# Hybrid attention and recurrence block on one core: f, q and k projected with the activations stationary and turned by transposing transfers

## The chip, the cores and the metric

The kernel runs on one core of a Trainium2 chip. Its time is the device time of one execution in microseconds, as the median of several runs. On the core, PE multiplies matrices, DVE and ACT work elementwise, POOL issues some transfers here, and SP does nothing but issue transfers, one after another. Each engine takes its instructions in the order of the program and waits at an instruction until what it needs is there.

## What is computed

One layer on 256 positions of 2048 channels, all in float32. Cut to what matters here:

```python
a = rmsnorm(h, norm_mix_pre)
proj = a @ w_in                  # q, k, v of 24 heads; q, f, i, g of 8 recurrent heads; 2 gates
qh, kh = rotary(q), rotary(k)    # per head of 128: x * cos + [-x[64:], x[:64]] * sin
attn = dilated window attention in three groups of 8 heads, mixed by their softmax denominators
f = lb + (1 - lb) * sigmoid(f_r); q_h = silu(q_r)
r_out = gated linear recurrence(q_h, log f, 1 - f, i_r), normed, gated
y = sigmoid(gate_a) * (attn @ w_attn_branch) + sigmoid(gate_r) * (r_out @ w_hgrn_branch)
h = h + rmsnorm(y @ w_mix_out)
h = h + rmsnorm((silu(gate) * up) @ w_ffn_down)
```

## The kernel before

Every float32 matrix product is made of three products of halves: weight and activation are split into a high part (a rounded copy, ACT) and a low part (the rest, DVE), and high x high, high x low and low x high are added up in PSUM. The normed input lies transposed in SBUF as `xT` (channels on partitions, tokens along the row), its two parts side by side.

The weights come as a stream that a list of items orders, and one loop walks the list. An item of the first stage ("wide": g, the gates, v, i) holds 1 MB of weights. An item of the second stage is a chunk of 512 KB; two chunks are loaded into one `raw` buffer by `load_pair` (two transfers on SP). There are three `raw` buffers and three `w` buffers for the split weights. In its turn of the loop, item i does this: `prepare(i)` splits the weights of item i+2 (`split_chunk`: ACT copies the high part, DVE subtracts) and asks for a load further on; `multiply(i)` issues the matmuls; `advance(evacs)` moves the evacuation of the last finished block by one step, up to its next `yield`; `advance_lanes()` does a step of the recurrence and of the attention, which run beside the stream; `ahead_of_time(i)` issues a piece of `weight_sums`, which lays sums of weights for the feed-forward part into DRAM, by POOL. With three `w` buffers, the split of a chunk can start when PE has finished the chunk three places before it; PE then has two chunks ready.

The second stage is f, q of the recurrence, and q and k of the attention: 16 blocks of 512 columns (f twice, recurrent q twice, then for each half of the heads q and k of three groups). A block of kind "W" has the weights stationary: its product comes out transposed, with channels on partitions and tokens along the row, as recurrence and attention want them. The moving operand is `both`, high and low part of the activations together, 512 wide, and then the high part alone, 256 wide, against the low weights. Each block of 512 columns is two of 256 (`add_wide`), and `both_halves` adds the two halves of its bank. `evac_rope` then swaps halves of the partitions (ACT) and multiplies by tables that stand along the partitions. The other kind, "N", has the activations stationary and 512 columns of weights moving; the later gates and the two branches use it.

The feed-forward part already turns matrices by transposing transfers: `turn_act` splits float32 words into their 16-bit halves (ACT, L1387), lets SP transpose them (L1393), and joins the halves again two steps later (ACT, L1402).

Of the kernel before, what the change touches and what calls it, by code (L numbers as in the profile page):

```python
# [14 lines left out]
F32 = mybir.dt.float32  # L15
# [37 lines left out]
class Block:  # L53
# [7 lines left out]
    def __init__(self, kind, w, nk, col, xs, evac, pre=None, mid=None, post=None):  # L61
        self.kind, self.w, self.nk, self.col = kind, w, nk, col
# [39 lines left out]
def tile_hybrid_block(ctx: ExitStack, tc: tile.TileContext, t, out):  # L102
# [81 lines left out]
    rowb = cpool.tile([P, S], F32, name="rowb")  # L184
# [9 lines left out]
    tabs = kp.tile([P, 4, S], F32, name="tabs")  # L194
# [37 lines left out]

    def add_wide(w, nk, col, xs, ev, post=None):
        for i in range(2):
            add("W", w, nk, col + 256 * i, xs, both_halves(ev, i), post=post if i == 0 else None)

    def both_halves(ev, i):
        def go(banks):
            s = ptile("sum").rearrange("p (h t) -> p h t", h=2)
            for n, ps in enumerate(banks):  # L240
                nc.scalar.activation(s[:, n, :], ps[:, S:], AF.Copy)
            for n, ps in enumerate(banks):
                nc.vector.tensor_add(s[:, n, :], ps[:, :S], s[:, n, :])
            yield from ev(i, s)
        return go
# [50 lines left out]
    def weight_sums(jobs):  # L296

        def pieces(n):
            b, i = steps[n][:2]
            m = b.order[i][0]  # L300
            return [
                b.w[(2 * m + k) * P : (2 * m + k + 1) * P, b.cols[g] : b.cols[g] + 512]
                for g, k in product(range(2), repeat=2)
            ]

        def copy(n, lo):
            if lo == 0:
# [14 lines left out]
        for at in range(len(jobs) + 3):  # L322
            for lag in (3, 2, 1, 0):
                for part in stages[lag]:
                    if 0 <= at - lag < len(jobs):
                        part(jobs[at - lag])
                    yield
            yield
            yield
# [61 lines left out]
    def multiply_chunk(j, sides=(0, 1)):  # L391
# [4 lines left out]
        for s in sides:  # L396
            if s == 1 and c == 0 and b.mid:
                b.mid()
            for kk in range(b.per):
                k = b.per * c + kk  # L400
                first, last = k == 0, k == b.nk - 1
                xh, xl, both = b.xs(k)
                if b.kind == "N":
                    ps = b.banks[s]
                    sh, sl = (x[:, s * P : (s + 1) * P] for x in (xh, xl))
                    mm(ps, sh, wh[:, kk, :], first, False)
                    mm(ps, sh, wl[:, kk, :], False, False)
                    mm(ps, sl, wh[:, kk, :], False, last)
                    continue
                h, l = (w[:, kk, s * P : (s + 1) * P] for w in (wh, wl))  # L410
                pair = [(b.banks[s], h, both), (b.banks[s][:, :S], l, xh)]
                for i, (ps, x, y) in enumerate(pair if k % 2 == 0 else pair[::-1]):
                    mm(ps, x, y, first and i == 0, last and i == 1)
# [156 lines left out]

    class Split:
# [77 lines left out]
    def row_broadcast(dst, rc):  # L649

        ds = [small("diag", P, 2) for _ in range(2)]
        for b in range(2):
            nc.vector.tensor_scalar(ds[b], ident, rc[:, b : b + 1], None, op0=OP.mult)
        yield
        yield
        yield
        ps = aux()
        for b in range(2):
            mm(ps[:, b * P : (b + 1) * P], ones[:, :P], ds[b], True, True)
        yield  # L660
        nc.scalar.activation(dst, ps[:, :S], AF.Copy)

    def by_rows(row, n):
        return row[:, None, :].to_broadcast([P, n, S])

# [51 lines left out]
    def opening():  # L717
# [8 lines left out]
        yield from row_broadcast(rowb, r1c)  # L726
        ready.add("rowb")
        yield
        for _ in range(24):
            yield  # L730
        for i, (j, c) in enumerate(((0, -QSCALE), (1, QSCALE), (0, 1.0), (1, -1.0))):
            nc.vector.scalar_tensor_tensor(
                out=tabs[:, i, :], in0=cs[:, j, :], scalar=c, in1=rowb, op0=OP.mult, op1=OP.mult
            )
            yield
# [58 lines left out]
    def evac_f(half):  # L794
        def ev(i, src):
            while "lb" not in ready:
                yield
            if i == 0:
                fT[half] = fslot("f").rearrange("p (h t) -> p h t", h=4)
            dst = fT[half]  # L800
            d = dst[:, 2 * i : 2 * i + 2, :]
            nc.vector.tensor_mul(d, src, by_rows(rowb, 2))
            nc.scalar.activation(d, d, AF.Sigmoid)
            yield
            for h in (2 * i, 2 * i + 1):
                g = 4 * half + h
                nc.vector.tensor_scalar(
                    dst[:, h, :], dst[:, h, :], lb1[:, g : g + 1], lb[:, g : g + 1],
                    op0=OP.mult, op1=OP.add,
                )  # L810
        return ev

    def evac_qr(half, then=None):
        def ev(i, src):
            if i == 0:
                qT[half] = fslot("q").rearrange("p (h t) -> p h t", h=4)
            d = qT[half][:, 2 * i : 2 * i + 2, :]
            s = ptile("sig").rearrange("p (h t) -> p h t", h=2)
            nc.vector.tensor_mul(d, src, by_rows(rowb, 2))
            nc.scalar.activation(s, d, AF.Sigmoid)  # L820
            yield
            nc.vector.tensor_mul(d, d, s)
            if i == 1 and then:
                then()
        return ev
# [69 lines left out]
    def evac_rope(key, tab, then=None):  # L895

        cos = tabs[:, tab, :]
        sin = tabs[:, tab + 1, :]

        def ev(i, src):  # L900
            if i == 0:
                qkT[key] = fslot("qk").rearrange("p (h t) -> p h t", h=4)
            yield
            w = ptile("w").rearrange("p (h t) -> p h t", h=2)
            for o, n in ((0, 64), (64, 0)):
                nc.scalar.activation(w[o : o + 64], src[n : n + 64], AF.Copy)
            yield
            u = src
            nc.vector.tensor_mul(u, src, by_rows(cos, 2))
            nc.vector.tensor_mul(w, w, by_rows(sin, 2))  # L910
            nc.vector.tensor_add(
                qkT[key][:, 2 * i : 2 * i + 2, :].rearrange("p h (two j) -> p h two j", two=2),
                u.rearrange("p h (j two) -> p h two j", two=2),
                w.rearrange("p h (j two) -> p h two j", two=2),
            )
            if i == 1 and then:
                then()
        return ev
# [667 lines left out]
    for half in range(2):  # L1586
        add_wide(w_in, KD, COL_FR + 512 * half, xT, evac_f(half),
                 post=(lambda c: end_phase0() if c == 2 else None) if half == 0 else None)
    for half in range(2):
        add_wide(w_in, KD, COL_QR + 512 * half, xT,  # L1590
                 evac_qr(half, start_recurrence(half)))
    for half in range(2):
        for g in range(3):
            c = 1024 * g + 512 * half
            add_wide(w_in, KD, COL_Q + c, xT, evac_rope(("q", half, g), 0))
            if g == 2:
                items_pre[len(chunks)] = lambda half=half: fetch_values(half)
            add_wide(w_in, KD, COL_K + c, xT, evac_rope(("k", half, g), 2,
                     start_attention(half) if g == 2 else None))
# [3 lines left out]
    for j in range(2, 4):  # L1603
        add("N", w_in, KD, COL_GA + 512 * j, xT, evac_gate(("a", j)))
    for j in range(4):
        add("N", t["w_hgrn_branch"][0], 8, 512 * j, lambda k: recT[0](k), evac_rec_branch(j),
            pre=begin_branches if j == 0 else None)
    for j in range(4):
        add("N", t["w_attn_branch"][0], 8, 512 * j, lambda k: attnT[0](k), evac_attn_branch(j),
# [141 lines left out]
```

## Time and profile before

| what | number |
|---|---|
| median of three runs | 1689.33 us (1688.76 to 1690.47) |
| the profiled execution | 1692.25 us, its span 1690.5 us |
| granted clock of PE, mean | 0.999 |
| PE busy | 1677.3 us, 99% of the span |
| DVE busy | 1367.4 us, 81% |
| ACT busy | 982.9 us, 58% |
| moved by transfers | 419.31 MB |

A share of busy time is an average over stages. The second stage lies from 350 us to 756 us of the span. Idle time of an engine that others do not wait for costs nothing.

### The profile page before, as it was taken

Reading aid. Unit: us, or ns where it says so; the run is one execution under the profiler, and the core shown is the slowest. Engines: PE = TensorE matmul, PEld = TensorE weight load, DVE = VectorE, ACT = ScalarE, POOL = GpSimd, SP = SyncE. Lnnn points to the kernel's source line nnn. Section 1 sums busy time; section 2 is a strip of 40 time slices with the busy share of each in tenths; the row PEclk is TensorE's granted clock in tenths of the full one; section 3 lists DMA queues with packets and bytes.
Section 4 is the critical chain, followed back from the end, with each engine's and each line's share of the span. In section 5 each row is a group of like instructions: output and inputs, shape, how many; then the busy total and the mean of one; then the engine's idle time right before and its main releaser. Section 6 shows DMA issues by size and latency. Waiting matters only on the chain.

```text
span 1690.5 us, 22175 instructions
## 1 busy us (share of the span) xinstructions
PE 1677.3 (99%) x8169; PEld 1406.0 (83%) x8169; DVE 1367.4 (81%) x1543; ACT 982.9 (58%) x1102; POOL 199.9 (12%) x358
## 2 busy tenths in 40 slices
PE   9999999999999999999999999999999999999997
PEld 7888878888888888888888888888888888888886
DVE  6999888865876876665568988899888888898987
ACT  6655555544455545555545556676667666665653
POOL 0012222143443332210000000000000000000000
PEclk9999999999999999999999999999999999999999
DMA  8678989999999998865657556899888888887673
GB/s 286 206 249 279 272 270 272 272 270 254 282 247 243 297 247 214 213 219 171 218 181 265 192 194 197 271 288 269 270 265 284 273 272 273 278 275 271 238 254 131
DMA packets 257006, 419.31 MB, mean 248 GB/s; under 512 B 38352, under 2 KB 105088, under 8 KB 256896
## 3 DMA queue, kind: packets, MB, share of 16 engines
q1 hardware_dynamic: 231600, 358.73, 65.6%
q0 software_dynamic: 17984, 41.97, 12.4%
q10 hardware_dynamic: 7312, 17.18, 2.8%
q8 instruction: 64, 1.05, 0.3%
q14 instruction: 46, 0.38, 0.1%
HBM read 397.89 MB, written 56.10 MB: 269 GB/s over the span
## 4 chain that ended last, share of the span: by engine, by line
PE 83%; DMA 7%; DVE 4%; ACT 3%; issue 2%; POOL 1%; ACTq 0%; SPq 0%; DVEq 0%; POOLq 0%
PE acc L139 55%; PE aux L139 27%; DMA raw<-in_w_in 7%; DVE wl L434 2%; ACT w L432 1%; DVE e L534 1%; ACT dh L459 1%; PE aux L962 0%; POOL beats L343 0%; ACT e L849 0%; PE aux L629 0%; DVE sum L448 0%; DVE fz L1525 0%; DVE w L379 0%; ACTq L852 0%
## 5 line engine op out<-in xcount | busy, mean ns | idle before, releaser
L139 PE MATMUL acc<-xT,w 128*128 128x256 f32 (+1 forms) x2048 | 365.4, 338 | 0.2 <-DVE w L379 0.2
L434 DVE TENSOR_TENSOR wl<-raw,w 128x2048 fp32r<-128x2048 f32 (+1 forms) x140 | 304.4, 2183 | 74.3 <-ACT w L432 72.5
L379 DVE TENSOR_TENSOR w<-raw,w 128x1024 fp32r<-128x1024 f32 x176 | 215.3, 1224 | 166.7 <-ACT w L378 166.6
L139 PEld LDWEIGHTS acc<-xT,w 128*128 128x128 f32 x2048 | 311.9, 188 | 45.2 <-DVE w L379 0.6
L432 ACT ACTIVATE w<-raw 128x2048 fp32r<-128x2048 f32 (+1 forms) x140 | 254.5, 1826 | 104.2 <-DMA raw<-in_w_in 27.6
L378 ACT ACTIVATE w<-raw 128x1024 fp32r<-128x1024 f32 x176 | 186.0, 1058 | 195.3 <-PE acc L139 144.3
L139 PE MATMUL acc<-w,xT 128*128 128x512 f32 x578 | 168.9, 392 | 0.0
L453 ACT ACTIVATE w<-sum 128x1024 fp32r<-128x1024 f32 x57 | 60.6, 1063 | 168.7 <-DVE sum L448 159.0
L343 POOL COPY beats<-raw 128x1 f32<-128x1 f32 x185 | 92.2, 499 | 523.5 <-DMA raw<-in_w_in 522.9
L139 PE MATMUL acc<-w,hT 128*128 128x512 f32 x472 | 152.7, 391 | 0.4 <-DVE hT L1276 0.4
L461 DVE TENSOR_TENSOR wl<-sum,w 128x1024 fp32r<-128x1024 f32 x114 | 137.2, 1221 | 6.8 <-ACT w L453 6.7
L139 PEld LDWEIGHTS acc<-w,xT 128*128 128x128 f32 x578 | 108.2, 188 | 22.2
L139 PE MATMUL aux<-w,hT 128*128 128x512 f32 x374 | 120.0, 389 | 0.0
L139 PE MATMUL aux<-w,xT 128*128 128x512 f32 x344 | 109.9, 389 | 0.0
L463 DVE TENSOR_TENSOR dl<-raw,dh 128x1536 fp32r<-128x1536 f32 x57 | 100.2, 1757 | 11.0 <-ACT dh L459 9.4
L139 PEld LDWEIGHTS acc<-w,hT 128*128 128x128 f32 x472 | 88.5, 188 | 19.0 <-DVE hT L1276 0.9
L139 PE MATMUL acc<-wl,hT 128*128 128x512 f32 x236 | 91.8, 389 | 0.0
L459 ACT ACTIVATE dh<-raw 128x1536 fp32r<-128x1536 f32 x57 | 84.1, 1475 | 5.0 <-PE acc L139 3.2
L139 PE MATMUL acc<-w,a 128*128 128x512 f32 x268 | 83.6, 389 | 0.0
L139 PEld LDWEIGHTS aux<-w,hT 128*128 128x128 f32 x374 | 70.2, 188 | 14.5
L139 PE MATMUL acc<-w,so 128*128 128x512 f32 x240 | 80.4, 389 | 0.0
L139 PE MATMUL aux<-w,a 128*128 128x512 f32 x254 | 79.5, 389 | 0.0
(289 smaller groups left out, 3115.8 us busy)
## 6 DMA issues: line engine op xcount, KB each, us to landing
raw<-in_w_in SPq DMA_DIRECT2D x270, 512.0 KB, 6.6
raw<-in_w_ffn_gate_up SPq DMA_DIRECT2D x156, 512.0 KB, 5.1
raw<-in_w_ffn_down SPq DMA_DIRECT2D x88, 512.0 KB, 5.5
presum<-in_w_ffn_gate_up POOLq DMA_DIRECT2D x120, 256.0 KB, 6.8
s<-presum SPq DMA_DIRECT2D x40, 512.0 KB, 6.7
raw<-in_w_mix_out SPq DMA_DIRECT2D x32, 512.0 KB, 4.9
act<-acts SPq DMA_DIRECT2D x22, 512.0 KB, 6.4
presum<-presum POOLq DMA_DIRECT2D x40, 256.0 KB, 6.5
```

What stands on the lines that cost most here:

```text
L139: nc.tensor.matmul(ps, lhsT, rhs, start=start, stop=stop, skip_group_check=True)
L343: nc.gpsimd.tensor_copy(beats, ahead[:, :1])
L378: nc.scalar.activation(wh, raw, AF.Copy)
L379: nc.vector.tensor_sub(wl, raw, wh.bitcast(F32))
L432: nc.scalar.activation(hi[:, c], raw[:, c], AF.Copy)
L434: nc.vector.tensor_sub(lo[:, c], raw[:, c], hi[:, c].bitcast(F32))
L453: nc.scalar.activation(hi[:, :1024], s[:, :1024], AF.Copy)
L459: nc.scalar.activation(dhi, d, AF.Copy)
L461: nc.vector.tensor_sub(lo[:, c], s[:, c], hi[:, c].bitcast(F32))
L463: nc.vector.tensor_sub(dlo, d, dhi.bitcast(F32))
L534: add_to(b.rest[key], b.bank[key], b.rest[key])
```

## The change

All 16 blocks become kind "N", so the kind goes, with `add_wide`, `both_halves`, `row_broadcast` and the row `rowb`. A block is one of 512 columns now, in eight chunks. It comes out with tokens on partitions, so evacuation works along the row: `side` applies sigmoid, or the rotation, to 128 tokens by 512 columns, and the result is turned. For this `halves_apart` (ACT) lays the 16-bit halves of the words apart, two transposing transfers on SP turn them (one per 128 tokens), and after some yields `halves_joined` (ACT, twice) puts words together. The tables of the rotation are transposed at the start and scaled per token. `weight_sums` loses two empty steps per round, and its steps are taken at each item of the first stage, at two of five chunks at first and at every second later, until the mixing begins.

```diff
-        self.per = 4 if kind == "W" else 2
-        self.width = 1024 // self.per
+        self.per, self.width = 2, 512
...
     def ahead_of_time(i):
 
-        if back:
+        first = len(early) * KD // 2
+        turn = items[i][0] is steps or (i % 5 in (0, 2) if i < first + 8 * KD else i % 2 == 0)
+        if back and turn and i < together:
...
+    def halves_apart(flat, words):
+
+        nc.scalar.activation(
+            flat.bitcast(U16).rearrange("p (z c) -> p z c", z=2),
+            words.bitcast(U16).rearrange("p (c z) -> p z c", z=2), AF.Copy,
+        )
...
+    def by_channel(side, done, parity=False, turns_for=3):
+
+        def go(banks):
             while "lb" not in ready:
                 yield
...
+            for i in range(2):
+                halves_apart(flat[:, i, :], side(i, banks[i]))
+            for i in range(2):
+                nc.sync.dma_start_transpose(
+                    planes.rearrange("p (n t) -> p n t", n=8)[:, :, i * P : (i + 1) * P],
+                    flat[:, i, :].bitcast(U16),
+                )
+            for _ in range(turns_for):
+                yield
+            words = fslot("words")
...
+                halves_joined(words, planes.rearrange("p (z n) -> p z n", z=2))
+            done(words.rearrange("p (h t) -> p h t", h=4))
+        return go
...
+    def evac_f(half):
+        def side(i, ps):
+            d = ptile("d")
+            nc.scalar.activation(d, ps, AF.Sigmoid, scale=r1c[:, i : i + 1])
+            return d
...
+    def evac_qr(half, then):
+        def side(i, ps):
+            d, r = ptile("d"), r1c[:, i : i + 1]
+            nc.scalar.activation(d, ps, AF.Sigmoid, scale=r)
+            nc.vector.scalar_tensor_tensor(
+                out=d, in0=ps, scalar=r, in1=d, op0=OP.mult, op1=OP.mult
+            )
+            return d
...
     def evac_rope(key, tab, then=None):
...
+            nc.vector.tensor_mul(u, x, by_heads(tabs[:, tab, i, :]))
+            nc.vector.tensor_mul(w, x, by_heads(tabs[:, tab + 1, i, :]))
             for o, n in ((0, 64), (64, 0)):
...
+                nc.vector.tensor_sub(u[:, :, o : o + 64], u[:, :, o : o + 64], w[:, :, n : n + 64])
+            return u.rearrange("p h d -> p (h d)")
...
+        return by_channel(side, done, True, 2 if then else 3)
```

`then` starts the attention and is given for the last k block of each half; these two blocks are joined one chunk earlier. In the changed kernel the split is at L362 (ACT) and L363 (DVE), `load_pair` at L255, the rotation at L915 to L918, `halves_apart` at L550, the transposes at L792, `halves_joined` at L564.

On ACT, before, around the first q block of the attention's second half (`sum` is what `both_halves` adds, `w` of L906 the swapped halves, `p` and `pt` the attention's):

```order
L378 ACTIVATE w_5206<-raw_4995 128x1024
L378 ACTIVATE w_5239<-raw_5060 128x1024
L241 ACTIVATE sum_5263<-acc_5115 128x256
L241 ACTIVATE sum_5263<-acc_5116 128x256
L950 ACTIVATE p_5273,m_5274<-p_5273,m_5274 128x512
L378 ACTIVATE w_5279<-raw_5060 128x1024
L906 ACTIVATE w_5298<-sum_5263 64x512 x2
L378 ACTIVATE w_5305<-raw_5112 128x1024
L378 ACTIVATE w_5346<-raw_5112 128x1024
```

The evacuation stands in pieces of two between the copies of the splits. On ACT, now, at the same block (`flat` are the halves apart, `turn` the transposed ones, `words` the joined):

```order
L362 ACTIVATE w_4855<-raw_4665 128x1024
L362 ACTIVATE w_4870<-raw_4724 128x1024
L550 ACTIVATE flat_4890<-u_4892 128x1024
L550 ACTIVATE flat_4890<-u_4899 128x1024
L362 ACTIVATE w_4928<-raw_4724 128x1024
L957 ACTIVATE p_4947,m_4948<-p_4947,m_4948 128x512
L362 ACTIVATE w_4951<-raw_4783 128x1024
L362 ACTIVATE w_4971<-raw_4783 128x1024
L564 ACTIVATE words_4986<-turn_4891 128x1024 x2
L362 ACTIVATE w_5007<-raw_4832 128x1024
```

Both `flat` stand ahead of the copy of the next chunk but one (`w_4928`), and `words` stands ahead of `w_5007`. When `flat` is made PE has left the block; `w_4870`, `w_4928`, `w_4951`, `w_4971`, `w_5007` are the third to the seventh chunk of the block after it.

On DVE, now, at the same place (`u` and `w` of L915 to L918 belong to the rotation, `acc` is the finished bank):

```order
L363 TENSOR_TENSOR w_4870<-raw_4724,w_4870 128x1024
L915 TENSOR_TENSOR u_4892<-acc_4668,tabs 128x512
L916 TENSOR_TENSOR w_4893<-acc_4668,tabs 128x512
L918 TENSOR_TENSOR u_4892<-u_4892,w_4893 128x4x64 x2
L915 TENSOR_TENSOR u_4899<-acc_4669,tabs 128x512
L916 TENSOR_TENSOR w_4900<-acc_4669,tabs 128x512
L918 TENSOR_TENSOR u_4899<-u_4899,w_4900 128x4x64 x2
L363 TENSOR_TENSOR w_4928<-raw_4724,w_4928 128x1024
```

The whole rotation of a block stands between two splits, where before it was three operations for half a block. On SP, now, with what each waits for (DVE_49 is a count of DVE's instructions):

```order
L255 DMA raw_4832<-in_w_in 128x2x512 [waits DMAHW1_49,DMAHW2_49,DVE_49,Pool_49]
L255 DMA raw_4832<-in_w_in 128x2x512
L255 DMA raw_4873<-in_w_in 128x2x512 [waits DMAHW5_49,DMAHW3_49,DMAHW6_49,DVE_49,Pool_49]
L255 DMA raw_4873<-in_w_in 128x2x512 [waits DMAHW4_49]
L792 DMA_TRANSPOSE turn_4891<-flat_4890 128x8x128 x2
L255 DMA raw_4954<-in_w_in 128x2x512 [waits DMAHW7_49,DMAHW0_49,DVE_49]
```

Before, this queue holds loads alone here. `raw_4873` takes the buffer of `raw_4724`, so its first transfer waits until DVE has split both chunks of that buffer, `w_4928` the last; the two transposes stand behind it, and they have no wait of their own, since that one contains it.

More of the change, by code (lines that the diff above doesn't have):

```diff
@@ L231, in add @@
             chunks.append([b, c, None, None, None])
[L233 to L245, printed above, removed]
     def add_wide_block(*args, **kw):
@@ L327, in weight_sums @@
                     yield
-            yield
-            yield
     def fetch_sums(i):
@@ L401, in multiply_chunk @@
                 first, last = k == 0, k == b.nk - 1
[L402 to L413, printed above, removed]
+                ps = b.banks[s]
+                sh, sl = (x[:, s * P : (s + 1) * P] for x in b.xs(k)[:2])
+                mm(ps, sh, wh[:, kk, :], first, False)
+                mm(ps, sh, wl[:, kk, :], False, False)
+                mm(ps, sl, wh[:, kk, :], False, last)
     def split_wide(n):
@@ L568, in pair_sums, with halves_joined @@
             yield
+    def halves_apart(flat, words):
[3 more added lines that the diff above has]
+        )
+    def halves_joined(words, planes):
+        n = len(words.shape)
+        for z in range(2):
+            out = words.bitcast(U16)
+            if n == 2:
+                out = out.rearrange("p (c z) -> p z c", z=2)[:, z, :]
+            else:
+                out = out.rearrange("p h two (j z) -> p z h two j", z=2)[:, z]
+            nc.scalar.activation(out, planes[:, z], AF.Copy)
     class Split:
@@ L647, in transpose_in @@
         high(0), high(1), low(0), low(1)
[L649 to L664, printed above, removed]
     evacs, turns, lanes, queue = deque(), deque(), [deque(), deque()], deque()
@@ L725, in opening @@
         nc.scalar.preload_act_table_set("silu_and_others")
-        yield from row_broadcast(rowb, r1c)
-        ready.add("rowb")
+        for _ in range(5):
+            yield
+        ps = aux()
+        for j, i in product(range(2), repeat=2):
+            nc.tensor.transpose(
+                ps[:, (2 * j + i) * P : (2 * j + i + 1) * P], cs[:, j, i * P : (i + 1) * P], ident
+            )
         yield
-        for _ in range(24):
+        nc.scalar.activation(cs, ps.rearrange("p (j t) -> p j t", j=2), AF.Copy)
+        for _ in range(22):
             yield
[L731 to L734, printed above, removed]
+        for n, (j, c) in enumerate(((0, -QSCALE), (1, QSCALE), (0, 1.0), (1, -1.0))):
+            for i in range(2):
+                nc.vector.tensor_scalar(
+                    tabs[:, n, i, :], cs[:, j, i * P : (i + 1) * P], r1c[:, i : i + 1], c,
+                    op0=OP.mult, op1=OP.mult,
+                )
             yield
@@ L792, in tile_hybrid_block @@
     fT, qT, gN, iN = {}, {}, {}, {}
-    def evac_f(half):
-        def ev(i, src):
+    def by_channel(side, done, parity=False, turns_for=3):
+        def go(banks):
             while "lb" not in ready:
                 yield
[L798 to L805, printed above, removed]
+            flat, planes = (
+                fp[0].tile([P, 1024], F32, tag="t", bufs=2, name=nm(n)) for n in ("flat", "turn")
+            )
+            flat, planes = flat.rearrange("p (s n) -> p s n", s=2), planes.bitcast(U16)
+            for i in range(2):
+                halves_apart(flat[:, i, :], side(i, banks[i]))
+            for i in range(2):
+                nc.sync.dma_start_transpose(
+                    planes.rearrange("p (n t) -> p n t", n=8)[:, :, i * P : (i + 1) * P],
+                    flat[:, i, :].bitcast(U16),
+                )
+            for _ in range(turns_for):
+                yield
+            words = fslot("words")
+            if parity:
+                halves_joined(
+                    words.rearrange("p (h two j) -> p h two j", h=4, two=2),
+                    planes.rearrange("p (z h j two) -> p z h two j", z=2, h=4, two=2),
+                )
+            else:
+                halves_joined(words, planes.rearrange("p (z n) -> p z n", z=2))
+            done(words.rearrange("p (h t) -> p h t", h=4))
+        return go
@@ L806, in ev, with done @@
+    def evac_f(half):
[3 more added lines that the diff above has]
+            return d
+        def done(f):
+            fT[half] = f
+            for h in range(4):
                 g = 4 * half + h
                 nc.vector.tensor_scalar(
-                    dst[:, h, :], dst[:, h, :], lb1[:, g : g + 1], lb[:, g : g + 1],
+                    f[:, h, :], f[:, h, :], lb1[:, g : g + 1], lb[:, g : g + 1],
@@ L809, in ev @@
                     op0=OP.mult, op1=OP.add,
                 )
[L811 to L825, printed above, removed]
+        return by_channel(side, done)
@@ L827, in totals, with done @@
+    def evac_qr(half, then):
[4 more added lines that the diff above has]
+                out=d, in0=ps, scalar=r, in1=d, op0=OP.mult, op1=OP.mult
+            )
+            return d
+        def done(q):
+            qT[half] = q
+            then()
+        return by_channel(side, done)
     def totals(b, then):
@@ L895, in evac_rope, with side, by_heads, done @@
     def evac_rope(key, tab, then=None):
[L897 to L904, printed above, removed]
-            for o, n in ((0, 64), (64, 0)):
[L906 to L916, printed above, removed]
+        def side(i, ps):
+            def by_heads(x):
+                return x[:, None, :].to_broadcast([P, 4, P])
+            u, w = (ptile(n).rearrange("p (h d) -> p h d", h=4) for n in ("u", "w"))
+            x = ps.rearrange("p (h d) -> p h d", h=4)
+            nc.vector.tensor_mul(u, x, by_heads(tabs[:, tab, i, :]))
+            nc.vector.tensor_mul(w, x, by_heads(tabs[:, tab + 1, i, :]))
+            for o, n in ((0, 64), (64, 0)):
+                nc.vector.tensor_sub(u[:, :, o : o + 64], u[:, :, o : o + 64], w[:, :, n : n + 64])
+            return u.rearrange("p h d -> p (h d)")
+        def done(x):
+            qkT[key] = x
+            if then:
                 then()
-        return ev
+        return by_channel(side, done, True, 2 if then else 3)
     attnT, recT = [], []
```

26 lines of the change are left out of this document (12 added, 14 removed).

## The prediction

> **What bounds the kernel now.** I read the page's busy times and slices first, then a table by stages, then the groups by form, then the queue of SP, and last one turn of the feed-forward part in order of time.
>
> ```profile
> PE 1677.3 (99%) x8169; PEld 1406.0 (83%) x8169; DVE 1367.4 (81%) x1543; ACT 982.9 (58%) x1102; POOL 199.9 (12%) x358
> PE   9999999999999999999999999999999999999997
> ...
> 56.00:350.00 294.00, 292.11 (x1280) 239.32 (x1279) 255.99 (x229) 160.25 (x133) 60.50 (x98) 1.00 0.84 260
> 350.00:443.00 93.00, 92.85 (x532) 80.65 (x531) 60.77 (x77) 46.69 (x63) 36.22 (x64) 1.00 1.04 269
> 443.00:755.00 312.00, 312.00 (x1943) 276.69 (x1942) 226.99 (x338) 167.50 (x268) 99.27 (x182) 1.00 0.90 245
> 1450.00:1690.00 240.00, 231.18 (x1019) 190.76 (x1017) 213.34 (x240) 141.87 (x147) 0.00 (x0) 0.99 0.70 236
> ```
>
> The last four rows give length, busy time of PE, weight loads, DVE, ACT and POOL, then granted clock, share of the DMA engines, GB/s. PE never rests in the stage that is changed: 312.00 of 312 us. So every microsecond of matmul taken away there is a microsecond won, and every wait that is new is lost in full. DVE and ACT have room on the average (227 and 168 of 312), but they work in order, and PE can wait for them.
>
> **The matmuls.** Pieces of the chain of waits in which PE does one thing only give the pace of each form, and the line of all matmuls gives the stage:
>
> ```profile
> 350.08 19.52 PE acc L139 x112
> 855.58 24.50 PE acc L139 x108
> ...
> L139 PE MATMUL acc<-xT,w x2048: 274/386/497, 349.9 to 755.6; 128*128 128x512 f32 x94, 128*128 128x256 f32 x93
> ```
>
> Kind W: 19.52/112 = 0.1743 us per matmul, alternately 512 and 256 wide. Kind N: 24.50/108 = 0.2269 us at 512. A block of 512 columns had 128 of the first, 22.31 us, and gets 96 of the second, 21.78 us: 0.53 us won, 8.5 us over 16 blocks. The same rows move; what goes is the fixed part of 32 matmuls. A chunk of N is 12 matmuls, 2.72 us. From 443 to 755 us at least 2048 - 532 = 1516 of the 1943 matmuls are the stream's, 264 us; the other 48 us, over 95 chunks, are recurrence and attention (the lanes): 0.5 us per chunk.
>
> **The evacuation: busy time.** Groups by form, mean of one:
>
> ```profile
> L378 ACT ACTIVATE w<-raw 128x1024 fp32r<-128x1024 f32 x176 | 186.0, 1058 | 195.3 <-PE acc L139 144.3 <-issue 22.1 <-DMA raw<-in_w_in 7.0
> L906 ACT ACTIVATE w<-sum 64x512 f32<-64x512 f32 x48 | 30.3, 632 | 1.2 <-DVE sum L243 0.3
> L241 ACT ACTIVATE sum<-acc 128x256 f32<-128x256 f32 x64 | 20.5, 372 | 0.0
> L849 ACT ACTIVATE e<-e,r1c 128x512 f32<-128x512 f32 x24 | 17.2, 716 | 4.9 <-ACT e L849 4.9
> L1387 ACT ACTIVATE e<-e x20: 1037/1042/1061, 1093.1 to 1471.3; 128x1024 uint16<-128x1024 uint16 x20
> L1402 ACT ACTIVATE act<-e x20: 1338/1352/1380, 1105.3 to 1484.3; 128x1024 uint16<-128x1024 uint16 x20
> L379 DVE TENSOR_TENSOR w<-raw,w 128x1024 fp32r<-128x1024 f32 x176 | 215.3, 1224 | 166.7 <-ACT w L378 166.6
> L243 DVE TENSOR_TENSOR sum<-acc,sum 128x256 f32<-128x256 f32 x64 | 24.0, 416 | 0.0
> L909 DVE TENSOR_TENSOR sum<-sum,tabs 128x512 f32<-128x512 f32 x24 | 16.4, 685 | 0.0
> L1484 DVE SCALAR_TENSOR_TENSOR fz<-e,r2c,fpost 128x512 f32<-128x512 f32 x8 | 6.0, 749 | 0.1
> ...
> 601.93 0.69 DVE L909 TENSOR_TENSOR sum<-sum,tabs 128x512 f32<-128x512 f32 x1
> 602.54 0.69 DVE L910 TENSOR_TENSOR w<-w,tabs 128x512 f32<-128x512 f32 x1
> 603.26 0.69 DVE L911 TENSOR_TENSOR qk<-sum,w 128x512 f32<-128x512 f32 x1
> ```
>
> A rotary block cost ACT 4 x 0.372 + 4 x 0.632 = 4.0 us and DVE 4 x 0.416 + 6 x 0.685 = 5.8. Now ACT has two L550 (as L1387) and two L564 (as L1402), 4.8, and DVE four products and four differences, 4 x 0.685 + 4 x 0.416 = 4.4. So the amounts hardly move. What moves is where it stands: in one lump, with ACT and DVE waiting for each other, and a transfer in between that ACT waits for. The three starts show that neighbours on DVE begin 0.61 apart (0.08 less than they last), or 0.72 where the next needs the result: a side of the rotation is 0.61 + 0.72 + 2 x 0.34 = 2.01 us.
>
> **The turn.** Before, it exists only in the feed-forward part, with four transposes of half our width: the same 512 KB. Three of nine turns there, SP and ACT in order of time (start, length):
>
> ```profile
> 1134.78 0.90 SPq L289 DMA_DIRECT2D raw<-in_w_ffn_gate_up  x2
> 1135.77 6.73 SPq L1393 DMA_TRANSPOSE e<-e  x4
> 1257.29 7.13 SPq L1393 DMA_TRANSPOSE e<-e  x4
> 1338.89 6.12 SPq L1393 DMA_TRANSPOSE e<-e  x4
> ...
> 1144.31 2.58 ACT L1402 ACTIVATE act<-e 128x1024 uint16<-128x1024 uint16 x2 [1.23 <-DMA e<-e]
> 1147.36 1.06 ACT L453 ACTIVATE w<-sum 128x1024 fp32r<-128x1024 f32 x1 [0.46 <-ACT act L1402]
> 1267.62 2.58 ACT L1402 ACTIVATE act<-e 128x1024 uint16<-128x1024 uint16 x2 [3.02 <-DMA e<-e]
> 1346.61 2.59 ACT L1402 ACTIVATE act<-e 128x1024 uint16<-128x1024 uint16 x2 [0.41 <-DMA e<-e]
> ```
>
> From SP's first transpose to the join that waited for them: 1135.77 to 1144.31 is 8.54 us, the longest 10.33, the shortest 7.72. I take 7.7: two instructions in place of four, and a stage in which loads come more slowly once PE waits. It is hardly much under 5.5, since SP alone was at it for 6.1 and more and the landing comes behind; were its work per instruction and not per byte, half of 6.12 is 3.1 us, and 7.72 - 6.12 = 1.6 us of landing, twice at most, comes on top: 4.7 to 6.3. From the join's start to the next copy is 1147.36 - 1144.31 = 3.05 us.
>
> **The path that sets the end, in a rotary block.** T is when ACT starts the copy of the third chunk of the next block, which PE's end of this one releases. In the order of the queues:
> - copy 1.06, subtraction 1.22: T+2.28
> - the rotation of both sides, 2 x 2.01: T+6.30
> - the second `flat` 1.04: T+7.34
> - the fourth chunk's copy and subtraction, which stand behind: T+9.62. PE comes there after 3 x (2.72 + 0.5) = T+9.66. Just in time: nothing.
> - SP's load of `raw_4873`, which waits for this subtraction, ahead of the transposes (0.90, and 0.09 to the next): T+10.61
> - the turn 7.72: T+18.33. ACT, done with the sixth chunk's copy at about T+10.7, has waited some 7.6 us at the join. Behind it stand the split of the seventh chunk and so PE.
> - join to next copy 3.05, copy and subtraction 2.28: the seventh chunk is ready at T+23.66. PE was there at T+19.3. It waits 4.3 us.
> - chunks seven and eight, 2 x 3.22: the block ends at T+30.1.
>
> Before, a block there took 22.31 + 8 x 0.5 = 26.3 us. So each of the ten rotary blocks costs 3.8 us more. The two that start the attention join one chunk earlier, so that the sixth chunk waits: 23.66 + 3 x 3.22 = 33.3, or 7.0 more.
>
> The f blocks need no DVE in between: copy 1.06, sigmoid 0.716, flat 1.04, sigmoid, flat: 4.57; split 2.28, load 0.99, turn 7.72, join 3.05, split 2.28: 20.89; two chunks without lanes 5.44: 26.3 against 22.3, 4.0 more. For the recurrent q, DVE's 0.749 comes in twice: 2.28 + 0.75 + 1.04 + 0.72 + 0.75 + 1.04 = 6.58, then the same way to 22.90, with two chunks 28.3 against 22.8 with some lanes: 5.5 more.
>
> Sum: 10 x 3.8 + 2 x 7.0 + 2 x 4.0 + 2 x 5.5 = 71 us, the 8.5 won being in it. The profiled execution took 1692.25; the median of the runs, 1689.33, is 2.9 lower. On the median: 1760.
>
> [...] The turn's row has 6.73 us of SP for 512 KB, 78 GB/s. [...]
>
> **Edits costed at nothing.** The opening: a few small operations of DVE and PE are exchanged for others, in a stage where DVE is busy 256 of 294 us and the tables are wanted 90 us later. The weight sums: eight transfers per round of six items in place of eight, so 52 items issue about 69 in place of 52.
>
> ```profile
> q0 software_dynamic: 17984, 41.97, 12.4%
> presum<-in_w_ffn_gate_up POOLq DMA_DIRECT2D x120, 256.0 KB, 6.8
> presum<-presum POOLq DMA_DIRECT2D x40, 256.0 KB, 6.5
> SPq L271 <- DVE w L379: 415.4, 82, 8.7
> ```
>
> 160 transfers took 12.4% of 1690.5 us, 1.3 us each; 17 more are 22 us, hidden in the 16% of 294 us that the engines have free (47 us). Without that cover 22 us would be the price, and late weights what PE waits for. In the second stage transfers fall from one per chunk to about a half; PE waited for none there, so that wins nothing. SP stood 415 us waiting for splits: it has the time for the transposes, which hold loads back some 7 us, and a load is wanted five chunks, 14 us, later and lands in 6.6 or so: nothing, but only just.
>
> **The rivals.**
> - All of it hidden, faster. Place: the join of each block. If the seventh chunk is ready before PE is there, only the 8.5 us remain: 1681. That needs the way from T to the seventh chunk 4.3 us shorter, so the turn within 3.4 us, or the lanes' matmuls at 1.2 us per chunk and not 0.5. For it: in the feed-forward part ACT waits at most turns and PE has not a gap. Against: there PE has two steps of 1 MB ahead, here two chunks of half a size, and 7.72 was the shortest of nine.
> - Transposes at the pace of plain transfers, or their cost per instruction. If SP's time goes by the instruction, the turn is 4.7 to 6.3 us (above): 3.0 to 1.4 less in each of 16 blocks, 48 to 23 us, so 1712 to 1737. [...] For it: two instructions in place of four. Against: the transfers run beside loads of 1 MB, and the three turns shown differ by 2.6 us at the same size.
> - PE slows in its gaps. The first matmuls of the program came from rest:
>
> ```profile
> L139 PE MATMUL aux<-warm 128*128 128x512 bf16 x14 | 5.5, 556 | 1.2 <-DVE warm L163 1.2
> ```
>
> 14 in 5.5 us are 0.39 each, 0.17 over the later pace. If each of 16 gaps cost that for the 12 matmuls behind it, 33 us come on top: 1793. For it: gaps of 3 to 4 us each, of which the profile before has none; its only stage with a clock under 1.00, the last, ends in 9 us without matmuls. [...]
> - That the change does not shorten the matmuls: other pieces of kind N run at 0.229, where 0.35 per block remain. That is 3 us less won, within the rest.
>
> **How the numbers follow.** The path as worked out (1737 to 1785): 0.52. Cheaper transposes (1690 to 1737): 0.22, a fifth of that within 0.2% of no change. Slowed clock (1785 to 1805): 0.14. All hidden: 0.12. So faster by over 0.2% is 0.12, within 0.2% (3.4 us, what a measurement of this kernel can tell from no change) 0.04, slower 0.84. The range leaves out the hidden case and the ends of the others: 1693 to 1797, which takes in turns from 3.5 us to 10.3 us (2.6 more in 16 blocks, 42 us).
>
> **What would show it.** Right: ACT waits for `turn` at the join about 7 us in each block, over 100 us in all; PE waits for the split's DVE line (L363) 4 us per block, 60 to 80 us in sum, always at the seventh chunk, or the sixth at two; the second stage is 470 to 480 us long where it was 406; chunks of N go at 0.227. Wrong: PE stays at 99% and ACT's wait at the join is under 3 us, or the transposes start ahead of the load that I put before them; a clock under 1.00 in the second stage speaks for the third rival; waits of PE for weights in the first stage mean that the cover of the sums was not there.

## The result, and the profile after

The changed kernel takes 1798.74 us (median of four runs, 1798.02 to 1806.38), the kernel before 1689.75 beside it: a ratio of 1.0656, with a 95% interval of 1.0626 to 1.0685. It is slower, as forecast, but by 109 us and not by 71, and it lies 1.7 us above the range.

The profiled execution is the longest of the four: 1806.38 us, its span 1804.6, 114.1 more than that of before; 5 us of what follows are therefore not in the 109 between the medians. Busy times and slices on the page of the changed kernel:

```profile
PE 1708.6 (95%) x7657; PEld 1399.7 (78%) x7657; DVE 1341.3 (74%) x1497; ACT 1001.3 (55%) x1054; POOL 180.5 (10%) x312
...
PE   9999999988798879988899999999999999999997
...
PEclk9999999999899898989999999999999999999999
```

PE has lost its unbroken row of nines in the changed stage, and its granted clock, which was full there, dips in the same place. The stage is best cut at two events: its first matmul, and the first matmul of the recurrence's branch, which follows it. The table by stages for the kernel before, cut there (length, busy time of PE, weight loads, DVE, ACT, POOL, then clock, DMA share, GB/s):

```profile
349.92:806.58 456.66, 456.51 (x2726) 400.93 (x2725) 315.53 (x450) 241.79 (x367) 137.30 (x249) 1.00 0.89 243
806.58:1690.50 883.92, 873.97 (x3921) 723.04 (x3919) 757.04 (x798) 543.96 (x539) 0.00 (x0) 1.00 0.76 245
```

And for the changed kernel:

```profile
355.10:919.83 564.73, 486.25 (x2213) 394.88 (x2212) 289.29 (x402) 259.61 (x319) 76.47 (x142) 0.93 0.73 194
919.83:1804.60 884.77, 874.42 (x3921) 722.99 (x3919) 756.81 (x798) 543.97 (x539) 28.94 (x46) 1.00 0.78 251
```

So 355.10 - 349.92 = 5.2 us were lost ahead of the stage, 564.73 - 456.66 = 108.1 in it, and 0.9 behind it. In the stage PE rests for 564.73 - 486.25 = 78.5 us where it rested for 0.2. It is also busy 29.7 us longer, with 512 matmuls fewer. Who is waited for, PE and then ACT (us in total, times, longest):

```profile
PE acc L138 <- ACT w L362: 45.5, 15, 6.5
PE aux L969 <- DVE p L963: 11.8, 5, 8.6
PE acc L138 <- DVE w L363: 11.4, 18, 0.9
PE aux L138 <- ACT words L564: 8.6, 1, 8.6
...
ACT words L564 <- DMA turn<-flat: 120.9, 16, 10.6
```

PE waits for splits (45.5 and 11.4 us), and the splits stand behind a join that waits for the turn, once per block. Besides, it stands twice for 8.6 us at matmuls of the attention: one of them needs the joined words, the other needs `p`, whose exponential stands behind a join on ACT. One rotary block in order of time (start, length; in brackets the idle time and what ended it); T is 597.10:

```profile
597.10 1.06 ACT L362 ACTIVATE w<-raw 128x1024 fp32r<-128x1024 f32 x1 [1.69 <-PE acc L138]
...
603.44 1.06 ACT L550 ACTIVATE flat<-u 128x1024 uint16<-128x1024 uint16 x1 [0.94 <-DVE u L918]
...
605.48 1.23 DVE L363 TENSOR_TENSOR w<-raw,w 128x1024 fp32r<-128x1024 f32 x1 [2.08 <-ACT w L362]
...
606.76 8.23 PE L138 MATMUL acc<-w,xT 128*128 128x512 f32 x35 [0.39 <-DVE w L363]
...
608.09 5.53 SPq L792 DMA_TRANSPOSE turn<-flat  x2
...
615.71 2.52 ACT L564 ACTIVATE words<-turn 128x1024 uint16<-128x1024 uint16 x2 [7.40 <-DMA turn<-flat]
618.09 1.98 ACT L362 ACTIVATE w<-raw 128x1024 fp32r<-128x1024 f32 x2
619.15 1.23 DVE L363 TENSOR_TENSOR w<-raw,w 128x1024 fp32r<-128x1024 f32 x1 [8.98 <-ACT w L362]
...
619.17 0.79 PE L138 MATMUL acc<-w,xT 128*128 128x512 f32 x1 [4.18 <-ACT w L362]
...
620.43 10.31 PE L138 MATMUL acc<-w,xT 128*128 128x512 f32 x35 [0.47 <-DVE w L363]
...
628.11 1.06 ACT L362 ACTIVATE w<-raw 128x1024 fp32r<-128x1024 f32 x1 [1.70 <-PE acc L138]
```

The transposes start at T+10.99 and the join at T+18.61, after a turn of 7.62 us; the seventh chunk is split at T+23.28, and PE has waited 4.18 us for its high part. The copy at 628.11 is the T of the next block. What follows that rest shows in the clock, the column before the last two (table by stages, three stretches of the changed kernel):

```profile
611.00:618.00 7.00, 3.99 (x18) 2.98 (x16) 0.00 (x0) 2.29 (x2) 0.00 (x0) 1.00 1.12 270
618.00:624.00 6.00, 4.36 (x9) 3.10 (x10) 4.10 (x4) 2.78 (x5) 1.02 (x2) 0.50 0.52 81
624.00:630.00 6.00, 6.00 (x26) 4.89 (x25) 5.10 (x6) 3.47 (x4) 2.01 (x2) 0.93 0.67 213
```

PE comes back at 619.17 at half its clock. Cut into stretches of 2 us, the stage shows twelve such periods, eight of them 6.8 us long and eleven behind rests of 2.85 to 8.6 us. Together they are 41 us of full clock withheld. PE's busy time in them, by the same table cut at their ends, is 58.7 us; at half the clock that is at most 29 us lost.

### The profile page after: what moved, and what is told of

Same layout as the page of the kernel before. It is cut to its first block, busy times and chain, and to the rows that moved or that the text cites. A ratio compares the mean times of both kernels' runs of the same rounds, so it can differ in the third digit from the quotient of the medians.

```text
span 1804.6 us, 21040 instructions
## 1 busy us (share of the span) xinstructions
PE 1708.6 (95%) x7657; PEld 1399.7 (78%) x7657; DVE 1341.3 (74%) x1497; ACT 1001.3 (55%) x1054; POOL 180.5 (10%) x312
## 5 line engine op out<-in xcount | busy, mean ns | idle before, releaser
L138 PE MATMUL acc<-w,xT 128*128 128x512 f32 x2114 | 561.4, 407 | 56.9 <-ACT w L362 45.5
L138 PEld LDWEIGHTS acc<-w,xT 128*128 128x128 f32 x2114 | 411.1, 196 | 156.5 <-ACT w L362 51.8
L363 DVE TENSOR_TENSOR w<-raw,w 128x1024 fp32r<-128x1024 f32 x176 | 212.9, 1223 | 271.3 <-ACT w L362 271.3
L362 ACT ACTIVATE w<-raw 128x1024 fp32r<-128x1024 f32 x176 | 181.8, 1052 | 141.5 <-PE acc L138 125.1
L327 POOL COPY beats<-raw 128x1 f32<-128x1 f32 x139 | 69.2, 498 | 873.7 <-DMA raw<-in_w_in 726.2
L440 DVE TENSOR_TENSOR dl<-raw,dh 128x1536 fp32r<-128x1536 f32 x57 | 100.2, 1757 | 10.2 <-ACT dh L436 8.4
L564 ACT ACTIVATE words<-turn 128x1024 uint16<-128x1024 uint16 x32 | 40.5, 1331 | 120.9 <-DMA turn<-flat 120.9
L138 PE MATMUL aux<-w,a 128*128 128x512 f32 x254 | 79.5, 389 | 0.0
L138 PE MATMUL acc<-wl,xT 128*128 128x512 f32 x193 | 75.4, 391 | 2.3 <-DVE wl L411 2.3
```

Of the source, the lines that this page charges most:

```text
L138: nc.tensor.matmul(ps, lhsT, rhs, start=start, stop=stop, skip_group_check=True)
L362: nc.scalar.activation(wh, raw, AF.Copy)
L363: nc.vector.tensor_sub(wl, raw, wh.bitcast(F32))
L440: nc.vector.tensor_sub(dlo, d, dhi.bitcast(F32))
L564: nc.scalar.activation(out, planes[:, z], AF.Copy)
```

## The experiments

The stages below are cut at the same two events as above. "Rest" is the stage's length less PE's busy time.

**Join two chunks later.**

```diff
-    def by_channel(side, done, parity=False, turns_for=3):
+    def by_channel(side, done, parity=False, turns_for=5):
...
-        return by_channel(side, done, True, 2 if then else 3)
+        return by_channel(side, done, True, 4 if then else 5)
```

> The changed kernel with the join asked for two chunks later (five steps after the transposes, four for the two blocks that start the attention). Theory, the late join: PE's gaps come from ACT waiting for the turn at the join with the seventh chunk's copy behind it, and the half clock comes from the gaps. Then ACT's 120.9 us of waiting at the join fall under 30, the second stage has a clock of 0.99 or more, and the time is 1689.3 - 8.5 + about 5 for the weight sums = 1686, at most 1700. Rival, the turn's transfers cost PE whatever stands behind them (they hold back the loads on SP and share the DMA engines): gaps of PE then name loads or the split, and the time stays over 1740.

Measured 1728.17 us (ratio to before 1.0237, 1.0221 to 1.0254): 71 us less than the changed kernel. The stage, and ACT's wait at the join:

```profile
354.55:839.83 485.28, 461.53 (x2205) 381.36 (x2204) 289.40 (x400) 263.14 (x319) 82.03 (x142) 0.98 0.86 227
...
ACT words L564 <- DMA turn<-flat: 30.9, 12, 8.1
```

Rest falls from 78.5 to 23.8 us, and busy time by 24.7 at nearly the same count of matmuls. The transposing transfers are all still there, so most of the loss was where they are waited for. The 1700 of the theory was missed, since 31 us of waiting stay at the join. The longest, 8.1 us, belongs to a turn that began at 431.0 and was joined at 444.8, 13.8 us later; transfers of the weight sums ran beside it.

**No turn.** The joins read the halves laid apart straight away, at the old place; the two transposing transfers are gone, so the turning is left out.

```diff
-            for i in range(2):
-                nc.sync.dma_start_transpose(...)
...
-                halves_joined(words, planes...)
+                nc.scalar.activation(words..., flat..., AF.Copy)   # twice
```

> The changed kernel without the two transposing transfers of each block: the words are joined straight from the halves laid apart, so the turning is left out and heads see tokens and channels exchanged; all else is the same, the place of the join too. Theory, the turn's latency is the cost: ACT has nothing to wait for at the join, PE's gaps and the half clock go, 1680 to 1695. Rival, the lump of evacuation work on DVE and ACT between two splits holds the stream by itself: PE still waits for the fourth or the seventh chunk and the time is over 1720.

Measured 1698.86 us (1.0057, 1.0042 to 1.0071):

```profile
353.72:812.22 458.50, 451.55 (x2213) 377.06 (x2212) 290.99 (x402) 261.43 (x319) 79.01 (x142) 1.00 0.77 221
```

The clock is full and 7 us of rest are left, though the rotation stands in the same lump between the same two splits. So the turn's latency carries the loss and the lump little. It ended 4 us above the theory's range, with the weight sums (next) in it. PE's busy time here, 451.55, is what the stage's matmuls take at full clock: 5.0 less than before. I use that number as the gain.

**The new spread of the weight sums alone**, in the kernel before:

```diff
-            yield
-            yield
...
+        first = len(early) * KD // 2
+        turn = items[i][0] is steps or (i % 5 in (0, 2) if i < first + 8 * KD else i % 2 == 0)
-        if back:
+        if back and turn and i < together:
```

> The kernel before with the new spread of the weight sums alone (the two empty steps per round gone, steps at every item of the first stage, fewer later). Theory: the first stage of the changed kernel is about 5 us longer because more sums run there than the DMA engines have room for, so 3 to 6 us more than before: 1692 to 1696. Rival, the prediction's nothing: within 1.5 us of before, and the 5 us belong to the opening (tables, transposes).

Measured 1695.29 us (1.0040, 1.0026 to 1.0055): 6.3 us, between 4.4 and 9.3. The stage ahead of the change ends later, and the second stage gains nothing:

```profile
0.00:353.03 353.03, 347.41 (x1526) 281.86 (x1526) 295.04 (x295) 197.29 (x196) 73.09 (x124) 1.00 0.87 271
353.03:809.26 456.23, 456.23 (x2725) 401.00 (x2724) 315.48 (x450) 241.87 (x367) 82.35 (x142) 1.00 0.80 221
```

**Transposes ahead of the load.** In a chunk's turn of the loop the next load is asked for after the step of the evacuation, not before it:

```diff
-            prepare(i)
+            prepare(i, wide)      # splits, but no load in the second stage
...
         advance(evacs)
+        if not wide:
+            load_ahead(i)
```

> The changed kernel with a chunk's load asked for after the step of the evacuation, so that the two transposes stand ahead of the load on SP that waits for the fourth chunk's split; nothing else. By the path of the prediction the transposes start 2.28 us (the split) and 0.99 us (the load) earlier. Theory, the join's latency is the path: PE's gap of 4.3 us in a rotary block falls to about 1.0, the half clock goes with it (rest under 1.7 us drew none), 16 times 3.3 plus some 34 us of clock less: 1710 to 1730. Rival, the turn is bound by the load of the DMA engines and not by its start: it takes the 3.3 us longer, and the time stays over 1775.

Measured 1718.04 us (1.0173, 1.0159 to 1.0186), 81 us less than the changed kernel by the order of two instructions on SP:

```profile
352.49:832.35 479.86, 460.10 (x2214) 381.17 (x2213) 290.43 (x402) 261.50 (x319) 82.09 (x142) 0.99 0.87 228
...
ACT words L568 <- DMA turn<-flat: 27.6, 11, 8.3
```

The theory's number held. That makes the load, and the split it waits for, a step of the path, as the prediction had put it.

**Both, then with the old sums, then with the rotation spread.** Three kernels built on each other: the two edits above together; the weight sums as in the kernel before; and a step of the loop between the two sides of an evacuation:

```diff
             for i in range(2):
+                if i:
+                    yield
                 halves_apart(flat[:, i, :], side(i, banks[i]))
```

> Both: transposes ahead of the load, and the join two chunks later (five steps, four for the two that start the attention). The later join alone left 30.9 us of ACT's wait at the join and took 1728. Theory: the 3.3 us of an earlier start take nearly all of that away, no half clock, 1697 to 1705, which is the kernel without transposes (1698.9) and a little more. Rival, transposes and loads disturb each other on the DMA engines: PE waits for splits whose weights are late, and the time stays over 1715.

> The former and the weight sums spread as in the kernel before (a step at every item, two of ten empty). Theory, the new spread costs 6 us in the first stage (the kernel before with it took 1695.3): 1691 to 1698. Rival, with the old spread a step of the sums runs beside every chunk of the second stage, and the turn, which took 13.8 us where sums ran beside it, is late again: 1705 to 1725. A third: without the sums' cost the shorter matmuls show at last, 1682 to 1687.

> The changed kernel with transposes ahead of the load, the join two chunks later, the old spread of the weight sums, and one chunk between the two sides of an evacuation, so that the rotation no longer stands as one lump between two splits. The same without the spread took 1703.1, with 10.8 us of PE's waits in the stage that are mostly for splits behind the lump. Theory: these waits go, 1692 to 1697; the floor is before less 5 us, since the matmuls of the stage without the turn took 451.55 us of PE against 456.51. Rival: the turn starts a chunk later and is joined late again, 1705 or more.

Measured 1705.32 (1.0104, 1.0086 to 1.0122), 1703.12 (1.0092, 1.0077 to 1.0106) and 1722.75 us (1.0205, 1.0186 to 1.0223). The first:

```profile
352.87:816.42 463.55, 452.74 (x2205) 377.06 (x2204) 289.74 (x400) 263.25 (x319) 86.41 (x145) 1.00 0.90 237
```

The two edits take away all but 10.8 us of rest and 1.2 of slowed matmuls. The first missed its range by 0.3 us, and none of the three expectations for the second held. Giving the sums their old place gave 2 us there, within the spread of the two kernels' runs, and not 6; whether that is their transfers, which then run beside the stage, was not tried. Of the rest left in the first, 5.6 us are waits for splits and 5.2 waits of the attention's transposes. Spreading the rotation made it worse by 20 us, as the rival said: the turn starts a chunk later, and ACT waits for it again:

```profile
ACT words L568 <- DMA turn<-flat: 15.5, 7, 5.3
```

No version beats the kernel before. The new matmuls have 5 us to give, and the best kernel of this form still rests more than that.

**PE kept at work in the gap.** Two kernels, with products of zeros added to the block's own bank ahead of the seventh chunk. The first puts 16 into every block from the second on (ahead of the sixth at the two early joins), the second fewer than the gap holds, in seven blocks:

```diff
+            if s == 0 and c == 6:
+                for _ in range({1: 10, 2: 10, 3: 14, 4: 10, 6: 6, 7: 12, 8: 10}.get(bi, 0)):
+                    mm(b.banks[0], warm[:, :P], warm, False, False)
```

> The changed kernel with 16 matmuls of zeros put ahead of the seventh chunk (the sixth at the two attention-starting blocks) of each block from the second on, so that PE works in the gap; they add zeros to the block's own bank. The waits of ACT stay. Theory, the clock is halved because PE rests 3 to 9 us: the periods of half clock (81.9 us in all) go except those after the gaps that are not filled (two of 8.6 us), the clock in 350 to 860 us rises from 0.93 to 0.98 or more, and the time falls by 20 to 35 us, to 1764 to 1779, though 256 more matmuls are issued. Rival, the clock costs nothing because PE waits for the splits anyway: the time is 1798 or more.

> The changed kernel with 6 to 14 matmuls of zeros ahead of the seventh chunk in seven of the blocks (second to fifth, seventh to ninth, the fifth block's successor left out), each fill 0.6 to 2.5 us shorter than the gap that the trace of the changed kernel has there, so that it takes no time of PE that is wanted. ACT's wait at the join stays. Theory, rest halves the clock and that lies on the path: seven of the twelve periods of half clock go, each worth 3.4 us less some 0.6 us that lie in the gap itself, and the time falls by 15 to 20 us, to 1779 to 1784. Rival, the half clock is not on the path (the splits would be late all the same): 1795 to 1802 with a higher clock.

Measured 1805.86 (1.0686, 1.0662 to 1.0711) and 1802.42 us (1.0669, 1.0654 to 1.0683): no gain, though the withheld clock fell from 41 us to 17 and to 31. The theory's times failed, and the rivals' came out, 1798 or more for the first and 1795 to 1802, missed by 0.4, for the second. The stage, of the first and of the second:

```profile
349.76:913.83 564.07, 522.12 (x2453) 407.96 (x2468) 289.29 (x402) 259.63 (x319) 78.43 (x144) 0.97 0.74 194
...
350.94:911.29 560.35, 495.56 (x2285) 396.45 (x2284) 289.11 (x402) 259.40 (x319) 76.60 (x142) 0.95 0.74 195
```

At 0.216 us each, their pace in the records, the 240 and 72 fills that the trace has records of are 52 and 16 us. Without them PE is busy 470 and 480 us, 16 and 6 less than in the changed kernel, but rest and fill together are 94 and 80 us where the rest was 78.5. So what the clock gave back came again as waiting. Two reasons can be seen, though not how much each counts: at 16 per block the fill is longer than some gaps, and in the second kernel gaps grew in blocks without a fill. By the starts of the transposes there, four blocks in which a half-clock period had been removed were 2.3 to 5.0 us shorter, and two unfilled ones behind filled ones 2.5 and 3.3 us longer; but unfilled blocks farther on differ from the changed kernel by -2.3 to +4.0 us too, so these differences alone settle nothing. Neither number prices the clock, and the next two leave the path alone.

**The rest by itself.** The kernel before, with nothing of the change, and PE made to wait for ACT: 16 rests of seven copies, or 48 rests of two.

```diff
+            if s == 1 and b.kind == "W" and j % 8 in (6,):        # (2, 5, 7)
+                mm(b.banks[1], warm[:, :P], warm, False, False)
+                for _ in range(7):                                # 2
+                    nc.scalar.activation(warm, warm, AF.Copy)
+                mm(b.banks[1], warm[:, :P], warm, False, False)
```

> The kernel before with nothing of the change in it, and 16 rests of PE put into the second stage, one per block of 512 columns in the middle of its seventh chunk: PE multiplies zeros, ACT copies that tile of zeros onto itself seven times, and PE waits for it and multiplies zeros again. By ACT's 0.6 to 0.7 us for 128 x 512 a rest is 4.2 to 4.9 us, 67 to 78 us in all. Theory, rest of that length halves the clock and the half clock is lost in full where PE is the bound: 16 times some 2.8 us more (6.83 us at half, less the part that lies in the rest), 45 us, so 1689 + 72 + 45 = 1806. Rival, half clock in the records costs no time (or refilling it costs none): 1756 to 1767.

> The same with 48 rests of two copies each, three per block, 1.3 to 1.6 us: 62 to 77 us in all, about the same sum. Theory: rests of 1.7 us and less drew no half clock in the changed kernel, so the time is before plus the rests alone, 1751 to 1766, at a clock of 0.99 or more. Rival: any rest draws it, then some 1800.

Measured 1806.56 (1.0699, 1.0684 to 1.0713) and 1800.10 us (1.0654, 1.0639 to 1.0668). The expectations had left out the time of the added matmuls themselves, 32 and 96 of some 0.216 us: 7 and 21 us. Long rests, page and waits:

```profile
PE 1713.3 (95%) x8185; PEld 1435.1 (80%) x8201; DVE 1368.7 (76%) x1543; ACT 1053.5 (58%) x1214; POOL 194.4 (11%) x358
...
PE acc L139 <- ACT warm L402: 79.1, 16, 5.3
```

Short rests:

```profile
PE 1701.8 (95%) x8230; PEld 1418.9 (79%) x8265; DVE 1369.2 (76%) x1543; ACT 1042.8 (58%) x1198; POOL 192.7 (11%) x358
...
PE acc L139 <- ACT warm L402: 81.7, 48, 2.8
```

The rests have nearly the same sum. PE's busy time grew by 1713.3 - 1677.3 = 36.0 us in the one and by 24.5 in the other. Of the added matmuls the trace has records of 16 and 61 (3.5 and 13.2 us; the others lie in the rests). Less these, PE was busy 32.5 us longer behind 16 long rests, 2.0 us each, and 11.3 us behind 48 short ones, 0.2 each. In the short kernel three of the rests drew a period of half clock of 3.4 us, at most 5.1 us of that; the other 6, 0.1 per rest, are no more than what the modelled end of a matmul adds where none follows (0.39 us against a pace of 0.17 to 0.23). The cost is shown, on a path where PE is the only bound: each long rest, of about 4.9 us, cost its own length and 1.9 us more, the short ones, of 1.44 to 2.76 us, hardly more than their length. The expected 2.8 us per rest was too much. The first kernel met the 1806 by luck, since that error is made up for by the forgotten matmuls and rests a little longer than expected. The second lay 34 us over its range: the forgotten matmuls, rests that were 5 us longer (some hold a matmul without a record), the three periods and those ends.

## Why the prediction was off

**The matmuls: -8.5 forecast, -5.0 measured** as PE's busy time in the kernel without the turn. It is the size of the last rival (3 us less won). Whether the pace or the modelled ends of matmuls before waits make the difference is open.

**The path: 79.5 us of waits forecast (71 and the 8.5), 78.5 measured.** In the block above T+6.30 was T+6.34 (the start of the second flat), T+9.62 for the fourth chunk was T+9.61, T+10.61 for the transposes T+10.99, the turn 7.72 was 7.62, ACT's wait 7.6 was 7.40 (120.9 in all, against over 100), the seventh chunk's T+23.66 was T+23.28, and PE's 4.3 was 4.18 and 0.47. Single blocks scatter: the two transposes held SP for 4.1 to 7.5 us, and the turn took 6.2 to 10.3 us over the sixteen blocks, 8.2 in the mean. That the sums agree so well is in part luck. Only 45.5 + 11.4 = 56.9 us are the waits for splits that the path had; 17.2 are the two waits of the attention's matmuls, which it did not have, and in some of the last six blocks PE hardly waited for a split at all. That the join is the place and the load ahead of the transposes a part of it was confirmed by the edits of those two, 71 and 81 us. So the rival by which all is hidden fell. So did the one with cheaper transposes. Its lower end, 1690, stands for transposes at the pace of plain transfers, and no run shows that pace: the turns took 6.2 to 10.3 us here, against 7.72 to 10.33 in the feed-forward part before.

**The clock: the step that failed.** The sum priced a gap at its length. The slower clock behind it was kept as a rival with 33 us and a chance of 0.14, as if the path came out one way or the other; the measured time lies in that rival's 1785 to 1805, which the stated range cut off at 1797. It was no alternative: all gaps of 2.85 us and more in this stage drew half clock, eleven in the changed kernel (up to 8.62 us) and sixteen in its variants (up to 8.81), and the sixteen long rests of about 4.9 us in the kernel before show it with no change at all. Measured, PE was busy 486.25 - 451.55 = 34.7 us longer for the same matmuls. At most 29 of it are the clock, by PE's 58.7 us in the twelve periods; the other 5 or so are about what the ends of matmuls ahead of some 40 waits come to, at 0.1 us each. In the block shown the slow matmuls lie on the path: from 620.43 to 630.59 PE does not rest, its 35 matmuls take some 2.2 us longer than at 0.227, and the copy at 628.11, the next T, waits for PE. 78.5 + 34.7 - 5.0 is 108.2, the stage's 108.1; the two agree by construction, since 34.7 and 5.0 are taken from the same kernel without the turn. In this account the 33 us belonged into the sum: 1793. The account is of what PE did, not of what each part alone would give back. With the fills there was less slow clock and no less time, so over the whole stage it is not excluded that without the slow clock much of it would have been waiting, and that the path was priced too low instead. How much is not settled.

**The weight sums: costed at nothing, 6.3 us measured** on the kernel before, and 5.2 in the profile above. The cover named for them, 47 us of free transfer engines in the first stage, was an average. The prediction named waits of PE in the first stage as its sign; they are there, for splits of weights, 5.5 us in the profile after against 1.4 in the one before. The median load there took 6.7 us to land, 6.2 before. By which loads the sums hold PE up is not shown.

With both terms the sum would have been 1760 + 33 + 6 = 1799, against 1798.7. That it fits so closely is luck: the smaller gain of the matmuls, the scatter of the turns and the waits of the attention stand against each other in it. The direction and the place, the join that waits for the turn, were right.

## What to carry to other kernels

Follow a moved operation through every queue that it stands in: here the order of a load and two transposes on SP, with the load waiting for a split, was worth 81 us, and waiting for the result two steps later 71. Where PE was the bound and a change makes it rest, price each rest with what the clock takes behind it, in the sum and not as a rival, and ask first how long the rest is: in the kernel before it took 1.9 us behind each rest of about 4.9 us, and at most 0.2 behind those of 1.44 to 2.76. A saving of 5 us in a stage with no slack leaves room for one small wait; the number to work out first is what the new form could win if everything else were hidden.

## What the runs showed of the hardware

Not every rest of PE draws the half clock. In the kernel before with short rests, 43 rests of 1.44 to 1.90 us drew none, three of four of 2.41 us did, and one of 2.76 did not (most of these rests hold an added matmul of some 0.2 us that has no record); in the changed kernel all rests from 2.85 us on did, and in the kernel with long rests all sixteen of about 4.9 us. Short rests close together can draw it too: one of the twelve periods of the changed kernel, at 723.9, stands behind rests of 0.88 and 0.76 us with one matmul between them, and the kernel with the rotation spread has one, at 484.0, behind 0.77 and 0.76. The expectation for the short rests, that rests of 1.7 us and less had drawn none, overlooked the first of these.

The periods of half clock last 3.4, 6.8 or 10.2 us, and the rest alone does not decide which: behind the sixteen equal long rests nine lasted 6.8 us and seven 3.4. Where PE was the only bound, 1.9 us were paid per long rest.

One turn of the same 512 KB with two transposes held SP for 4.1 to 7.5 us and took 6.2 to 10.3 us from start to join. The longest of the kernel with the later join took 13.8, with transfers of sums beside it; whether these were the reason is not shown.
